# Sixteen column chunks instead of twelve in the opening of a decoder layer

## The chip, the cores and the metric

The kernel runs on one core of one Trainium2 chip. The metric is the time on the device of one launch, in microseconds (us). The figures used for comparison are medians over runs; the profile is of one further execution, and its own time stands beside its span below.

## What is computed

One layer with a batch of one, 256 positions, 2048 channels: a SwiGLU feed-forward block, a pair of token mixers (retention and windowed attention) and a second SwiGLU block, each behind an RMSNorm whose scale, shift and gate come from a conditioning vector `c`; then one last RMSNorm. The change touches the first block and the conditioning. Cut to that:

```python
mod = (silu(c) @ w_ada + b_ada).reshape(b, 9, 2048)          # w_ada: 2048 x 18432
h = rms_norm(x, norm_ffn1) * (1 + mod[:, 1]) + mod[:, 0]
gate, up = split(h @ w_ffn1_gu)                              # 2048 x 11264
x = x + 0.5 * mod[:, 2] * ((silu(gate) * up) @ w_ffn1_down)  # 5632 x 2048
h = rms_norm(x, norm_mix) * (1 + mod[:, 4]) + mod[:, 3]
# ... token mixing (mod 5), second feed-forward block (mod 6, 7, 8), last norm
```

Everything is float32. All weights are read from HBM once, about 595 MB.

## The kernel before

**Products.** A float32 product is made of three matmuls in a shorter format: each operand is split into a high and a low half, and high x high, low x high and high x low are summed in PSUM (`products`, lines 335 to 344; lines 342, 343 and 344 are the three). The 256 positions are two halves of 128, so one block of 128 weight rows times one chunk of 512 columns takes six matmuls. The weights are split as they come (`split`, lines 346 to 353): ScalarE casts two blocks at a time to the high half `wh` (line 350), VectorE subtracts to get the low half `wl` (line 352). The pool of these halves has three buffers for each. A raw load of weights lands in one of four buffers of four blocks, 1 MB each (`raws`, line 105).

**Conditioning.** For each of the nine vectors of `mod` and each of 16 blocks of 128 channels, a row of `w_ada` (1 MB, laid out with the channel on the partitions) is loaded (`ada_load`, line 197) and multiplied and summed on VectorE against `silu(c)` (`ada_pass`, line 203; its instruction is line 206, followed by a short read of the accumulator). In the opening a row takes two passes over 1024 columns; later it takes four over 512 (`AQ`).

**Opening (lines 867 to 993).** The normed input can only be used block by block, as the rows for `mod` 1 and 0 arrive. So the 16 blocks are put into groups, with `bounds` (line 931) of 2, 3, 3, 4 and 4 blocks. In each group twelve column chunks (`chunks`, gate and up chunks in turn, `2 * EARLY` of them) are visited once: `visit` (line 947) loads the group's blocks of that chunk and multiplies. There is PSUM for two chunks at a time (four accumulator banks). So between groups a chunk's sums go to SBUF (`to_parts`, line 965): the first time as a copy on ScalarE (line 970), later as an add on VectorE (line 968). `part_of` (line 873) says where: four chunks in each of three 16 KB slots. The order of chunks turns round with each group, and the last two chunks of a group stay in PSUM. In the last group `swiglu_up` (line 641) adds the partial sums (lines 651, 652), applies SiLU and multiplies (655), and transposes the result on TensorE (`transpose_to`, line 477, eight transposes for each pair of chunks).

While one group is visited, the rows of the next one are loaded and passed (`group`, line 900, a generator advanced after the visits, line 984). Its end transposes the normed input of the new blocks on TensorE (line 919), modulates on ScalarE (591, 596), and VectorE makes the low half of the activations (597). These rows use two half-slots in turn (`ring`).

**After the opening.** `ffn_up` (line 667) does the other chunk pairs over all 16 blocks at once, pairs 6 to 9 of eleven with the transposition done by DMA from SyncE (`turn_by_dma`, lines 484 to 510), over plane buffers (`flat`, `back`). Then comes the down product, whose activations are split into the pair buffers (`pair_tile`, line 357). After every two-block piece a `tick` (line 294) lets the generator `conditioning` (line 243) take some steps: it loads rows of `mod` 2, 4 and 3, up to `ahead` passes early, and passes them. `set_pace` (line 288) gives the steps per tick: 192 passes over 150 half-steps.

**Order.** SyncE issues the loads in program order, each when its buffer is free. The other engines' order is made by a scheduler at build time from the program order, except in parts written out by hand at the end of each down product.

Of the kernel before, what the change touches and what calls it, by code (L numbers as in the profile page):

```python
# [25 lines left out]
KB = 4  # L26
EPS = 1e-6
RAWS = 4
EARLY = 6

RH, RDK, RDV = 8, 128, 256
QH, KVH, HD = 32, 8, 64
# [45 lines left out]
def layer_kernel(  # L78
# [153 lines left out]
    def two_rows():  # L232

        both = slot()
        turn = [both[:, :D], both[:, D:]]

        def place():
            turn.append(turn.pop(0))
            return turn[-1]

        return place

    def conditioning(outputs, place, ahead, behind):


        tiles = [(m, k) for m, _, _ in outputs for k in range(KD)]
        held = {}
        step = 0
        for m, gain, row in outputs:
            sums = ada_sums()  # L250
            for k in range(KD):
                for q in range(AQ):
                    for i in range(step // AQ, min((step + ahead) // AQ + 1, len(tiles))):
                        if i not in held:
                            held[i] = place()
# [31 lines left out]

    def set_pace(outputs, halves, place, ahead):
        assert next(pace["steps"], None) is None
        pace["steps"] = conditioning(outputs, place, ahead, pace["behind"])  # L290
        pace["rate"] = len(outputs) * KD * AQ / halves
        pace["due"] = 0.0

    def tick():
        pace["due"] += pace["rate"]
# [50 lines left out]
    def split(pool, tag, src, n, hi_engine="act"):  # L346
        k = src.shape[1]
        hi = pool.tile([P, 2, n], F32R, tag=tag + "h", name=nm(tag + "h"))[:, :k, :]
        lo = pool.tile([P, 2, n], F32R, tag=tag + "l", name=nm(tag + "l"))[:, :k, :]
        cast.append(nc.scalar.copy(hi, src).ins)  # L350
        del cast[:-1]
        nc.vector.tensor_sub(lo, src, hi.bitcast(F32))  # L352
        return hi, lo
# [516 lines left out]
    tiles = [slot(), part[0]]  # L870
    ring = [tiles[0][:, :D], tiles[0][:, D:]]

    def part_of(n):
        at = (n % 4) * NT * CH
        return [part[n // 4][:, at + t * CH : at + (t + 1) * CH] for t in range(NT)]

# [51 lines left out]
    r = [Root(ssq, t).all() for t in range(NT)]  # L928
    for t in range(NT):
        nc.vector.tensor_scalar(out=r[t], in0=r[t], scalar1=HALF, scalar2=None, op0=ALU.mult)  # L930
    bounds = (0, 2, 5, 8, 12, 16)
    groups = [range(a, b) for a, b in zip(bounds, bounds[1:])]


# [9 lines left out]
        )  # L944
        return raw

    def visit(n, ks, raw, ends, step=2):
        starts = n not in banks
        if starts:
            banks[n] = [acc_bank() for _ in range(NT)]  # L950
        for a in range(0, len(ks), step):
            b = min(a + step, len(ks))
            hl = slice(ks[a], ks[a] + b - a)
            wh, wl = split(wsp, "w", raw[:, a:b, :], CH)
            products(
                banks[n],
                held.hi[:, hl, :],
                held.lo[:, hl, :],
                wh,
                wl,  # L960
                starts and a == 0,
                b == len(ks) and ends,
            )

    def to_parts(n):
        for p, b in zip(part_of(n), banks.pop(n)):
# [3 lines left out]
                nc.scalar.copy(p, b)  # L970
        moved.add(n)

    for _ in group(groups[0]):
        pass
    for g, ks in enumerate(groups):
        final = g == len(groups) - 1
        order = chunks if g % 2 == 0 else chunks[::-1]
        coming = iter(()) if final else group(groups[g + 1])
        due = 0 if final else 2 * len(groups[g + 1])
        stay = () if final else order[-2:]  # L980
        for i, n in enumerate(order):
            visit(n, ks, load_blocks(n, ks), n not in stay)
            last = len(order) - 2
            for _ in range((i + 1) * due // last - i * due // last if i < last else i == last):
                next(coming, None)
            if n in stay:
                continue
            if not final:
                to_parts(n)
            elif n % 2:  # L990
                swiglu_up(
                    banks.pop(n - 1), banks.pop(n), tiles, n // 2, (part_of(n - 1), part_of(n))
                )
    gate = gate_row()
    tiles.append(slot())
    place = two_rows()
    set_pace([(2, None, 0.5), (4, 1, None), (3, None, None)], 150, place, AQ)
    ffn_up(held, gu, tiles, EARLY, turned=range(EARLY, DFF // CH - 1))
    gate_load(gate, 2)
    wi = w_in[0]  # L1000
# [394 lines left out]
```

## Time and profile before

| | us |
|---|---|
| median of three runs | 2407.24 |
| lowest and highest | 2407.22, 2407.5 |
| profiled execution, its own time | 2406.89 |
| its span in the trace | 2404.9 |

| Engine | busy, us | share of the span |
|---|---|---|
| TensorE, matmul (PE) | 2369.5 | 99% |
| TensorE, weight load (PEld) | 1937.5 | 81% |
| VectorE (DVE) | 1694.8 | 70% |
| ScalarE (ACT) | 1293.9 | 54% |

In the profile's views a line names the engine, the source line (L352), the operation, the tiles written and read, their shapes and a count. A digit of the forty slices is the busy share in tenths of one fortieth of the span, about 60 us. "[1.66 <-PE pa L343]" behind an instruction says that its engine stood idle for 1.66 us before it, and that the wait ended when TensorE's line 343 had written the tile `pa`. A row of the view of waits has the waiting instruction, what ended the wait, and then total us, number of waits and the longest. Busy time is an average over stages: what a stage is worth is read from that stage.

### The profile page before, as it was taken

The page shows a single profiled execution, that of the slowest core. Times are in us where ns is not written, and L with a number is a line of the kernel's source. Part 1 is how long each engine was busy: PE and PEld are TensorE (multiplying, and loading weights), DVE is VectorE, ACT ScalarE, POOL GpSimd, SP SyncE. Part 2 cuts the span into 40 slices and gives each one's busy share as a digit, 9 for nine tenths or more (in the row PEclk, how much of TensorE's full clock was granted, in tenths as well). Part 3 has the DMA queues.
Part 4 walks back from the last instruction along what each step waited for, and adds up shares of the span by engine and source line. Part 5 has one row for each costly group of instructions (what it writes and reads, how often), then busy time and mean ns, then how long its engine had stood idle before and what let it go on. Part 6 is the DMA issues. An engine that isn't in the chain of part 4 may idle for free. (4 is left out here: it accounts for less than half of the span.)

```text
span 2404.9 us, 28941 instructions
## 1 busy us (share of the span) xinstructions
PE 2369.5 (99%) x10678; PEld 1937.5 (81%) x10678; DVE 1694.8 (70%) x2720; ACT 1293.9 (54%) x1799; POOL 5.7 (0%) x14
## 2 busy tenths in 40 slices
PE   6999999999999999999999999999999999999998
PEld 4778888888788887778888888887888888888886
DVE  7898787778877668886766766768655555545656
ACT  6544545454546456665555554456445445454544
POOL 0000000000000000000000000000000000000000
PEclk9999999999999999999999999999999999999999
DMA  9988688998876687775679787765677877875563
GB/s 354 341 327 286 230 309 301 374 321 310 299 263 227 228 283 226 223 230 210 218 252 290 264 282 265 278 197 203 221 239 238 247 255 241 260 221 188 184 205 126
DMA packets 307183, 614.28 MB, mean 255 GB/s; under 512 B 72737, under 2 KB 73121, under 8 KB 288225
## 3 DMA queue, kind: packets, MB, share of 16 engines
q1 hardware_dynamic: 305538, 605.78, 74.8%
q0 software_dynamic: 928, 5.61, 0.6%
q8 instruction: 84, 1.38, 0.2%
q10 hardware_dynamic: 576, 1.05, 0.1%
q14 instruction: 57, 0.47, 0.1%
HBM read 595.06 MB, written 2.12 MB: 248 GB/s over the span
## 5 line engine op out<-in xcount | busy, mean ns | idle before, releaser
L352 DVE TENSOR_TENSOR wl<-raw,wh 128x1024 fp32r<-128x1024 f32 (+1 forms) x806 | 968.2, 1207 | 560.4 <-ACT wh L350 555.6
L350 ACT CAST wh<-raw 128x1024 fp32r<-128x1024 f32 (+1 forms) x806 | 837.3, 1041 | 950.4 <-PE pa L343 932.7
L342 PE MATMUL pa<-wh,hh 128*128 128x512 f32 x2192 | 856.3, 392 | 2.3 <-ACT wh L350 1.8
L343 PE MATMUL pa<-wh,hl 128*128 128x512 f32 x2192 | 855.9, 391 | 2.1 <-DVE hl L597 2.1
L344 PE MATMUL pa<-wl,hh 128*128 128x512 f32 x2192 | 784.3, 392 | 2.5 <-DVE wl L352 2.4
L343 PEld LDWEIGHTS pa<-wh,hl 128*128 128x128 f32 x2192 | 411.9, 188 | 89.9 <-issue 3.0
L342 PEld LDWEIGHTS pa<-wh,hh 128*128 128x128 f32 x2192 | 411.6, 188 | 90.1 <-issue 2.8
L344 PEld LDWEIGHTS pa<-wl,hh 128*128 128x128 f32 x2192 | 409.1, 188 | 92.5 <-DVE wl L352 6.5
L343 PE MATMUL pa<-wh,a 128*128 128x512 f32 x944 | 365.1, 389 | 0.0
L342 PE MATMUL pa<-wh,a 128*128 128x512 f32 x944 | 350.0, 391 | 1.1 <-ACT wh L350 0.5
L344 PE MATMUL pa<-wl,a 128*128 128x512 f32 x944 | 349.0, 390 | 1.5 <-DVE wl L352 1.4
L344 PEld LDWEIGHTS pa<-wl,a 128*128 128x128 f32 x944 | 177.0, 188 | 40.2 <-DVE wl L352 3.5
L342 PEld LDWEIGHTS pa<-wh,a 128*128 128x128 f32 x944 | 177.1, 188 | 39.7 <-DVE slot L1277 1.0
L343 PEld LDWEIGHTS pa<-wh,a 128*128 128x128 f32 x944 | 177.1, 188 | 36.6 <-DVE a L385 0.2
L206 DVE CUSTOM_DVE_ANT_0 slot<-slot,cact 128x512 f32<-128x512 f32 (+1 forms) x252 | 192.8, 814 | 15.7 <-DMA slot<-in_w_ada_dram 15.6
L206 DVE CUSTOM_DVE_ANT_0 raw<-raw,cact 128x512 f32<-128x512 f32 (+1 forms) x260 | 167.1, 695 | 44.6 <-DMA raw<-in_w_ada_dram 33.9
L385 DVE TENSOR_TENSOR a<-slot,a 128x512 fp32r<-128x512 f32 x118 | 80.7, 685 | 1.7 <-ACT a L384 1.7
L508 ACT COPY slot<-back 128x512 uint16<-128x512 uint16 x116 | 77.1, 766 | 0.0
L384 ACT CAST a<-slot 128x512 fp32r<-128x512 f32 x118 | 72.7, 618 | 0.0
L494 ACT COPY flat<-t 128x512 uint16<-128x512 uint16 x104 | 58.9, 618 | 4.9 <-DVE t L1182 4.9
L206 DVE DVE_READ_ACCUMULATOR2_ANT sums<- 128x1 f32 x512 | 42.3, 83 | 0.0
L968 DVE TENSOR_TENSOR slot<-slot,pa 128x512 f32<-128x512 f32 x56 | 35.8, 681 | 0.0
(197 smaller groups left out, 1171.6 us busy)
## 6 DMA issues: line engine op xcount, KB each, us to landing
raw<-in_w_ffn_gu_dram SPq DMA_DIRECT2D x152, 1024.0 KB, 5.4
raw<-in_w_in_dram SPq DMA_DIRECT2D x104, 1024.0 KB, 5.3
raw<-in_w_ffn_down_dram SPq DMA_DIRECT2D x88, 1024.0 KB, 5.2
slot<-in_w_ada_dram SPq DMA_DIRECT2D x76, 1024.0 KB, 7.4
raw<-in_w_ada_dram SPq DMA_DIRECT2D x64, 1024.0 KB, 5.1
raw<-in_w_ffn_gu_dram SPq DMA_DIRECT2D x24, 768.0 KB, 7.2
raw<-in_w_swa_branch_dram SPq DMA_DIRECT2D x16, 1024.0 KB, 5.2
raw<-in_w_ret_branch_dram SPq DMA_DIRECT2D x16, 1024.0 KB, 5.2
```

The lines of the kernel that those rows point to most:

```text
L206: nc.vector.tensor_tensor_reduce(out=w[:, at], in0=w[:, at], in1=cact[:, at], scale=1.0, scalar=0.0, op0=ALU.mult, op1=ALU.add, accum_out= ...
L342: nc.tensor.matmul(ps, ah[:, j, ts], wh[:, j, :], start=first, stop=False)
L343: nc.tensor.matmul(ps, al[:, j, ts], wh[:, j, :], start=False, stop=False)
L344: nc.tensor.matmul(ps, ah[:, j, ts], wl[:, j, :], start=False, stop=last)
L350: cast.append(nc.scalar.copy(hi, src).ins)
L352: nc.vector.tensor_sub(lo, src, hi.bitcast(F32))
L384: nc.scalar.copy(hi, v)
L385: nc.vector.tensor_sub(lo, v, hi.bitcast(F32))
L494: nc.scalar.copy(planes[:, i, :], words(src)[:, :, i])
L508: nc.scalar.copy(into[:, :, :, i], held["turned"][:, i])
L968: nc.vector.tensor_add(p, p, b)
```

## The change

- `EARLY` becomes 8: sixteen chunks (eight pairs) in the opening, and `ffn_up` begins with pair 8. Pairs 6 and 7 are thus transposed on TensorE and no longer by DMA.
- The groups have 2, 4, 5 and 5 blocks. A visit with more than four blocks makes two loads, of three blocks and of the rest, and three pieces of 2, 1 and 2 blocks.
- The partial sums of chunks 12 and 13 are held in the two pair buffers, those of 14 and 15 in the four `back` plane buffers.
- In the last group each piece is followed by a `tick`, at a rate that takes 32 passes, which is eight of the later 48 rows. These rows (and the ninth) are placed in the raw load buffers, and are asked for one pass ahead. After the opening the rows go to two half-slots as before, and the other 160 passes are spread over 117 half-steps.
- The order of chunks begins reversed, so that the last group runs forward.

```diff
-EARLY = 6
+EARLY = 8
...
-                    for i in range(step // AQ, min((step + ahead) // AQ + 1, len(tiles))):
+                    for i in range(step // AQ, min((step + pace["ahead"]) // AQ + 1, len(tiles))):
...
+        pace["ahead"] = ahead
...
+    beside = [pair_tile() for _ in range(2)]
+    behind = [[back.tile([P, CH], F32, tag="back", name=nm("back")) for _ in range(NT)] for _ in range(2)]
+
     def part_of(n):
+        if n >= 14:
+            return behind[n - 14]
+        if n >= 12:
+            return [beside[n - 12][:, t, :] for t in range(NT)]
...
-    bounds = (0, 2, 5, 8, 12, 16)
+    bounds = (0, 2, 6, 11, 16)
...
-    def visit(n, ks, raw, ends, step=2):
+    def visit(n, ks, ends, ticks=False):
...
-        for a in range(0, len(ks), step):
-            b = min(a + step, len(ks))
-            hl = slice(ks[a], ks[a] + b - a)
-            wh, wl = split(wsp, "w", raw[:, a:b, :], CH)
+        cut = len(ks) if len(ks) <= KB else 3
+        raw_of = [(load_blocks(n, part), part) for part in (ks[:cut], ks[cut:]) if part]
+        pieces = [
+            (raw[:, a : a + 2, :], part[a : a + 2])
+            for raw, part in raw_of
+            for a in range(0, len(part), 2)
+        ]
+        for raw, part in pieces:
+            a, b = part[0] - ks[0], part[-1] + 1 - ks[0]
+            hl = slice(part[0], part[-1] + 1)
+            wh, wl = split(wsp, "w", raw[:, : len(part), :], CH)
...
+            if ticks:
+                tick()
...
+    ROWS_FFN1 = [(2, None, 0.5), (4, 1, None), (3, None, None)]
+    row_ring = []
+
+    def place_row():
+        return row_ring[0]() if row_ring else raw_row()
...
-        order = chunks if g % 2 == 0 else chunks[::-1]
+        if final:
+            set_pace(ROWS_FFN1, 48 * 192 // 32, place_row, 1)
+        order = chunks if (len(groups) - g) % 2 else chunks[::-1]
...
-            visit(n, ks, load_blocks(n, ks), n not in stay)
+            visit(n, ks, n not in stay, final)
...
-    place = two_rows()
-    set_pace([(2, None, 0.5), (4, 1, None), (3, None, None)], 150, place, AQ)
+    row_ring.append(two_rows())
+    pace["rate"] = (192 - 32) / 117
+    pace["ahead"] = AQ
     ffn_up(held, gu, tiles, EARLY, turned=range(EARLY, DFF // CH - 1))
```

More of the change, by code (lines that the diff above doesn't have):

```diff
@@ L241, in two_rows, with conditioning @@
         return place
-    def conditioning(outputs, place, ahead, behind):
+    def conditioning(outputs, place, behind):
         tiles = [(m, k) for m, _, _ in outputs for k in range(KD)]
@@ L289, in set_pace @@
         assert next(pace["steps"], None) is None
-        pace["steps"] = conditioning(outputs, place, ahead, pace["behind"])
+        pace["steps"] = conditioning(outputs, place, pace["behind"])
         pace["rate"] = len(outputs) * KD * AQ / halves
         pace["due"] = 0.0
+        pace["ahead"] = ahead
     def tick():
```

## The prediction

> **What bounds the kernel now.** I read the page first, for the engines' shares and the forty slices.
>
> ```profile
> span 2404.9 us, 28941 instructions
> PE 2369.5 (99%) x10678; PEld 1937.5 (81%) x10678; DVE 1694.8 (70%) x2720; ACT 1293.9 (54%) x1799; POOL 5.7 (0%) x14
> PE   6999999999999999999999999999999999999998
> PEld 4778888888788887778888888887888888888886
> DVE  7898787778877668886766766768655555545656
> ```
>
> TensorE (PE) sets the time nearly everywhere. Its row of nines hides small gaps, since the ends of matmuls are modelled; the weight-load row below it dips to 7 in slices 2 and 3 (60 to 180 us), just where VectorE (DVE) reads 8, 9 and 8. That is the opening, which the change rebuilds. So I next cut the opening into its five block groups.
>
> The cut comes from the timeline of ScalarE (ACT). The high-half buffers are three deep, so the cast of a piece waits for the last product of the piece three before it. Counting the casts (12 pieces in the first group, 24 in each later one), the cast three after a group's last piece marks that group's end on TensorE.
>
> ```profile
> 26.77 0.79 PE L342 MATMUL pa<-wh,hh 128*128 128x512 f32 x1 [0.81 <-ACT wh L350]
> ...
> 63.76 1.05 ACT L350 CAST wh<-raw 128x1024 fp32r<-128x1024 f32 x1 [0.18 <-PE pa L343]
> ...
> 113.51 1.05 ACT L350 CAST wh<-raw 128x1024 fp32r<-128x1024 f32 x1 [0.51 <-PE pa L343]
> ...
> 170.08 2.19 ACT L350 CAST wh<-raw 128x1024 fp32r<-128x1024 f32 x2 [0.62 <-PE pa L343]
> ...
> 238.24 1.05 ACT L350 CAST wh<-raw 128x1024 fp32r<-128x1024 f32 x1 [1.67 <-PE pa L343]
> ...
> 308.39 1.05 ACT L350 CAST wh<-raw 128x1024 fp32r<-128x1024 f32 x1
> ...
> 322.88 1.06 ACT L350 CAST wh<-raw 128x1024 fp32r<-128x1024 f32 x1 [1.68 <-PE pa L343]
> 325.60 1.06 ACT L350 CAST wh<-raw 128x1024 fp32r<-128x1024 f32 x1 [1.66 <-PE pa L343]
> 328.32 1.06 ACT L350 CAST wh<-raw 128x1024 fp32r<-128x1024 f32 x1 [1.66 <-PE pa L343]
> ```
>
> The third group's end is the second cast of the merged row, which ends at 172.27 after 1.06 us and so began at 171.21. The last three rows give the floor: 5.44 us for two pieces of two blocks each. One **unit** (one 128-row block of one column chunk, six products) costs 1.361 us of TensorE. The view of busy time by stretch, one row for each group and one for what follows (length, then busy time and count of PE, PEld, DVE, ACT, POOL, then clock, DMA share, GB/s):
>
> ```profile
> 26.77:63.75 36.98, 35.79 (x148) 28.19 (x149) 31.50 (x46) 27.43 (x45) 0.00 (x0) 1.00 1.01 386
> 63.75:113.51 49.76, 49.56 (x220) 40.62 (x219) 44.81 (x70) 24.69 (x37) 0.00 (x0) 1.00 0.90 330
> 113.51:171.21 57.70, 53.05 (x225) 40.16 (x224) 55.17 (x90) 26.02 (x41) 0.00 (x0) 1.00 0.88 323
> 171.21:238.24 67.03, 67.03 (x300) 55.01 (x299) 60.06 (x85) 32.35 (x44) 0.00 (x0) 1.00 0.84 306
> 238.24:308.38 70.14, 70.14 (x332) 58.28 (x331) 56.27 (x83) 39.87 (x51) 0.00 (x0) 1.00 0.67 227
> ```
>
> Floors are 24, 36, 36, 48 and 48 units: 32.7, 49.0, 49.0, 65.3 and 65.3 us. The excess is 4.3, 0.8, **8.7**, 1.7 and 4.8 us, 20.3 in all. The third group holds the loss worth having, and there VectorE is busy 55.17 of 57.70 us. One of its visits (a visit is one chunk times one group's blocks), on VectorE's timeline:
>
> ```profile
> 128.13 1.28 DVE L968 TENSOR_TENSOR slot<-slot,pa 128x512 f32<-128x512 f32 x2
> 129.32 1.22 DVE L352 TENSOR_TENSOR wl<-raw,wh 128x1024 fp32r<-128x1024 f32 x1
> 130.46 1.22 DVE L206 CUSTOM_DVE_ANT_0 slot<-slot,cact 128x1024 f32<-128x1024 f32 x1
> 131.60 0.08 DVE L206 DVE_READ_ACCUMULATOR2_ANT sums<- 128x1 f32 x1
> 131.60 1.22 DVE L206 CUSTOM_DVE_ANT_0 slot<-slot,cact 128x1024 f32<-128x1024 f32 x1
> 132.75 0.08 DVE L206 DVE_READ_ACCUMULATOR2_ANT sums<- 128x1 f32 x1
> 132.75 0.69 DVE L352 TENSOR_TENSOR wl<-raw,wh 128x512 fp32r<-128x512 f32 x1
> 133.35 1.28 DVE L968 TENSOR_TENSOR slot<-slot,pa 128x512 f32<-128x512 f32 x2
> ```
>
> From start to start: two adds into partial sums 1.19, a two-block split 1.14, a one-block split 0.60, one conditioning row (two passes) 2.29; the loop is 5.22 us against 4.08 (three units) on TensorE. Eight rows fall on the first ten visits, so the mean is 1.74 + 1.19 + 0.8 x 2.29 = 4.76 us, 0.68 over; ten visits lose 6.8 of the 8.7 us. The waits of that group show the rest:
>
> ```profile
> PE pa L343 <- DVE hl L597: 2.1, 2, 1.7
> PE pa L344 <- DVE wl L352: 2.0, 4, 0.8
> DVE slot L206 <- DMA slot<-in_w_ada_dram: 3.2, 2, 2.2
> ```
>
> VectorE stood 2.2 us at a row not yet landed at the boundary, and the low half of the activations (L597), queued behind it, was late. The fourth group has the same work at four blocks: 2.28 + 1.19 + 1.83 = 5.30 against 5.44, 97%, and loses only about 0.8 us beside its eight transposes. **So a group stalls when its visits are too narrow for the fixed work of rows and adds.**
>
> **The change, part by part.** *Wider groups and more chunks.* VectorE's need per visit, the same way (rows over the first 14 of 16 visits):
> - two blocks: 1.14 + 8/14 x 2.29 = 2.45 against 2.72 us (before 1.14 + 0.6 x 2.29 = 2.51);
> - four blocks: 2.28 + 1.19 + 10/14 x 2.29 = 5.11 against 5.44, 94%;
> - five blocks in pieces of 2, 1, 2: 2.88 + 1.19 + 1.64 = 5.71 against 6.80, 84%.
>
> The overload is gone from every group: of the 8.7 us, about 0.7 (six transposes) stays, 8.0 goes. The adds number 3 x 14 x 2 = 84 writes, 32 of them ScalarE copies, so 52 adds for 56 before: nothing. The pair and plane buffers are untouched until the first DMA turn and the down product, so holding partial sums there costs nothing; if a turn had to wait for one, TensorE would not, since its result is read by the down product. SyncE's issue of two loads per five-block visit is covered by 6.8 us of products.
>
> *First group.* It asks DMA for 0.524 + 0.571 x 1.049 = 1.12 MB per 2.72 us, 413 GB/s (before 0.524 + 0.6 x 1.049 = 1.15 MB, 424) where 386 were moved. The deficit lasts 14 visits instead of 10. Bounds: nothing (the old deficit is part of the 4.3), or 14 x (1.12/0.386 - 2.72) = 2.5 us. I take **0.5 us** more than the 4.3 of now, as the missing 27 GB/s make 1.0 MB over 38 us, as the 38 GB/s of now do over 27 us.
>
> *The last group.* Eight pairs of chunks turn on TensorE instead of six, two fewer by DMA.
>
> ```profile
> 257.10 0.40 PE L343 MATMUL pa<-wh,hl 128*128 128x512 f32 x1
> 257.34 1.04 PE L477 MATMUL ps<-small_c,t 128*128 128x128 f32 x8
> 258.13 0.47 PE L344 MATMUL pa<-wl,hh 128*128 128x512 f32 x1
> ```
>
> Eight transposes push the next product from 257.33 to 258.13: 0.80 us. Two more pairs cost **1.6 us**, surely on the path. VectorE there also gets eight rows, at two short passes a visit:
>
> ```profile
> L651 DVE TENSOR_TENSOR t<-pa,slot 128x512 f32<-128x512 f32 x12 | 7.9, 687 | 2.7 <-PE pa L344 2.7
> L206 DVE CUSTOM_DVE_ANT_0 slot<-slot,cact 128x512 f32<-128x512 f32 x12 | 7.6, 685 | 0.0
> ```
>
> Three such operations (0.66) and two passes (0.63 + 0.08): 2.88 + 1.98 + 1.42 = 6.3 against 6.8 + 0.4, 87%. It fits, but is no longer slack: a split waits behind a pass, and a pass behind its row. The rows now take one of the four load buffers, in SyncE's order between the weights. The trace has such rows only later in the kernel:
>
> ```profile
> DVE raw L206 <- DMA raw<-in_w_ada_dram: 33.9, 27, 3.1
> raw<-in_w_ada_dram SPq DMA_DIRECT2D x64, 1024.0 KB, 5.1
> raw<-in_w_ffn_gu_dram SPq DMA_DIRECT2D x10, 1024.0 KB, 5.0
> raw<-in_w_ffn_gu_dram SPq DMA_DIRECT2D x24, 768.0 KB, 7.2
> ```
>
> VectorE waits for 64 such rows 33.9 us in 27 waits, 0.5 a row, at most 3.1. (The last two rows are weights: 225 to 280 us and 25 to 302 us, with the median time to landing at the end.) Bounds for eight rows: nothing, or 8 x 3.1 = 25 us, of which 16 x 0.9 = 14 is cover, so 11. I take **1.2 us**, the kinder end, because SyncE reaches a row's load about a visit ahead of its first pass, longer than the 5.0 us that a load takes from 225 us on, where the group moved 227 GB/s (the changed stage asks for 1.84 MB per 7.2 us, 255 GB/s).
>
> *Boundaries.* Three instead of four, but up to five blocks are modulated at each. Bounds: nothing (the last boundary of now), or the 2.1 us of the third group's, each. I take 0.8 for the four-block group and 0.4 for the next, as the fourth group's 0.8 at 97%.
>
> *Later.* Forty rows over 117 half-steps instead of 48 over 150: 1.37 passes per step against 1.28. That is 0.09 x 0.7 us more per 2.72 us, covered where VectorE has most to do:
>
> ```profile
> 650.00:700.00 50.00, 49.31 (x214) 39.98 (x215) 43.73 (x77) 25.05 (x35) 0.00 (x0) 1.00 0.81 295
> ```
>
> VectorE is still idle for an eighth of that stretch; nothing to 1 us, I take nothing. The 64 units moved into the opening cost 1.361 each on either side.
>
> **Sum.** Against 20.3: 8.0 and about 0.8 (the fourth group's stall) go; 0.5, 1.6, 1.2, 0.8 and 0.4 come, 4.5 in all: a gain of **4.3 us**. The span becomes 2400.6. The profiled execution took 2406.89 with its span of 2404.9, and the median is 2407.24, 2.3 over the span: **2402.9 us**.
>
> **A rule against it.** In the first group, whose weight loads are of 512 KB, the engines moved 386 GB/s; in the second, of 768 KB, 330. The Trainium skill ("DMA: Bandwidth & Descriptors", "Rules for kernel authors") asks for at least 1 MiB in one DMA for full bandwidth, and a five-block visit here is cut into 0.75 and 0.5 MiB. By the rows the smallest loads stood beside the highest rate, so the sum takes nothing for it; by the rule these loads land late, which is the slower rival below.
>
> **Rivals.**
> *The load buffers run short (slower).* With a row in one of four, a visit's first load waits for the buffer of the visit before, which is free once that visit's second piece is split. Its cast goes when the second piece of the visit before that ends, 4.08 us into 7.2; with the cast (0.6), the split (0.6) and one other vector operation ahead (1.2) the buffer is free at 6.5, 7.9 us before the load's own visit. Less a cast of 1.06 and a split of 1.14, 5.7 us remain for landing. At 5.0 all is well; at 7.2, as the 768 KB loads took where groups moved 323 to 386 GB/s, each of eight row periods loses 1.5: 12.0 us, less the 1.2 counted, so 10.8 lost against 4.3 won: **2414 us**. For it: the two landing times lie on both sides. Against: the stage asks for 255 GB/s only.
>
> *The stall moves to the boundaries (no change).* If late rows and late halves, not visit width, made the third group's loss, each of three boundaries costs about 2.7 us (8.0 over the third group's one is the extreme); 8 - 1.2 = 6.8 more than counted would leave 2410, half of it **2406**. For it: the 2.1 and 2.2 us rows. Against: 5.22 against 4.08 within the group.
>
> *Nothing new stalls (better).* The first group costs no more, last group and boundaries lose nothing, and the 0.7 us idle at 650 to 700 goes too: 4.3 + 2.9 + 0.7 = 7.9: **2399 us**.
>
> **How the numbers follow.** Forecast 0.52 (its own range 2400 to 2405), boundaries 0.20, better 0.13, buffers short 0.15. The range that leaves out about 2 in 10 is 2397 to 2411. I call 0.2%, 4.8 us, what a measurement can tell from none. Faster by that needs under 2402.4: the better case (0.13), nearly half of the forecast (0.25) and 0.02 of the boundary case, 0.40; slower, over 2412, most of the buffer case with a little beyond the boundary one, 0.14; the rest, 0.46.
>
> **What would show it.** In the changed trace: four groups near 48, 89, 110 and 116 us; in the four- and five-block groups casts that wait for TensorE every piece; VectorE under 95% in each; row waits of some tenths in the last group. Wrong, if a group's excess over its units is above 4 us past the first, if weights' casts wait for DMA in the last group (buffers short), or if L597 holds TensorE at boundaries.

## The result, and the profile after

The change makes the kernel slower, where a gain of 4.3 us was forecast.

| | before | after |
|---|---|---|
| median, us | 2407.37 (8 runs) | 2413.61 (8 runs) |
| lowest and highest, us | 2406.85, 2408.61 | 2409.72, 2417.31 |
| profiled execution, its own time, us | 2406.89 | 2413.91 |
| its span in the trace, us | 2404.9 | 2412.1 |

The ratio is 1.0027, with a 95% interval from 1.0018 to 1.0036. The runs also scatter more: 7.6 us between the extremes against 1.8.

Line numbers move by one behind line 29 and by more later: the three products are lines 343 to 345 here, the cast is 351, the low half 353. Two of the costliest groups on the page of the changed kernel (line, engine, operation, tiles, count, then busy us, mean ns, and idle time before them with what ended it):

```profile
L345 PE MATMUL pa<-wl,hh 128*128 128x512 f32 x2192 | 784.3, 392 | 8.1 <-DVE wl L353 7.9
...
L206 DVE CUSTOM_DVE_ANT_0 raw<-raw,cact 128x512 f32<-128x512 f32 (+1 forms) x292 | 187.4, 695 | 74.1 <-DMA raw<-in_w_ada_dram 63.4
```

TensorE's idle time before the third product rose from 2.5 to 8.1 us, nearly all of it for low halves, and VectorE's wait for rows in load buffers from 33.9 to 63.4. Where that is, the same cut by groups shows. The ends of the four groups, read from ScalarE's casts as in the prediction:

```profile
75.74 1.05 ACT L351 CAST wh<-raw 128x1024 fp32r<-128x1024 f32 x1 [0.18 <-PE pa L344]
...
163.88 1.05 ACT L351 CAST wh<-raw 128x1024 fp32r<-128x1024 f32 x1 [2.10 <-PE pa L344]
...
276.95 1.06 ACT L351 CAST wh<-raw 128x1024 fp32r<-128x1024 f32 x1 [1.45 <-PE pa L344]
...
401.32 1.04 ACT L351 CAST wh<-raw 128x1024 fp32r<-128x1024 f32 x1 [2.46 <-DMA raw<-in_w_ffn_gu_dram]
```

The last of them was released by a load and not by TensorE, so that end is an upper bound. By TensorE's own records the next piece's first product starts at 400.50; where a cast is released by TensorE the two lie 0.03 us apart, so the last group ends at 400.47. The view by stretch (columns as in the prediction):

```profile
26.57:75.74 49.17, 47.18 (x196) 37.04 (x197) 41.50 (x58) 35.91 (x57) 0.00 (x0) 1.00 1.00 382
75.74:163.88 88.14, 88.14 (x393) 72.72 (x392) 76.60 (x106) 40.65 (x52) 0.00 (x0) 1.00 0.84 309
163.88:276.94 113.06, 110.94 (x495) 91.21 (x494) 93.14 (x134) 53.32 (x76) 0.00 (x0) 1.00 0.78 277
276.94:401.32 124.38, 118.18 (x543) 95.93 (x542) 97.69 (x169) 62.84 (x83) 0.00 (x0) 1.00 0.73 251
```

The floors are 32, 64, 80 and 80 units of 1.3605 us (the prediction's 1.361): 43.5, 87.1, 108.8 and 108.8. The excess is 5.6, 1.1, 4.2 and **14.7 us** (15.5 up to the cast), 25.6 in all against 20.3 before. The overload of VectorE is gone as computed (it is busy 87% and 82% of the second and third group), but the last group has taken the loss. Its waits:

```profile
DVE raw L206 <- DMA raw<-in_w_ada_dram: 22.3, 7, 5.3
PEld pa L345 <- DVE wl L353: 8.6, 6, 3.0
PE pa L345 <- DVE wl L353: 6.2, 4, 2.6
```

VectorE waits seven times, 3.2 us each, for a row that has not landed, and TensorE then waits for the low half that is queued on VectorE behind the row's passes. One such place on VectorE, the wait of TensorE that follows, and the same time on SyncE:

```profile
297.28 1.82 DVE L353 TENSOR_TENSOR wl<-raw,wh 128x1024 fp32r<-128x1024 f32 x2
299.02 1.28 DVE L652 TENSOR_TENSOR t<-pa,slot 128x512 f32<-128x512 f32 x2
300.38 1.23 DVE L353 TENSOR_TENSOR wl<-raw,wh 128x1024 fp32r<-128x1024 f32 x1
306.23 0.69 DVE L206 CUSTOM_DVE_ANT_0 raw<-raw,cact 128x512 f32<-128x512 f32 x1 [4.62 <-DMA raw<-in_w_ada_dram]
...
308.07 0.69 DVE L206 CUSTOM_DVE_ANT_0 raw<-raw,cact 128x512 f32<-128x512 f32 x1
...
308.69 1.82 DVE L353 TENSOR_TENSOR wl<-raw,wh 128x1024 fp32r<-128x1024 f32 x2
...
309.96 0.73 PE L345 MATMUL pa<-wl,hh 128*128 128x512 f32 x2 [1.88 <-DVE wl L353]
```

```profile
299.13 0.34 SPq L201 DMA_DIRECT2D raw<-in_w_ada_dram  x1
301.63 11.60 SPq L949 DMA_DIRECT2D raw<-in_w_ffn_gu_dram  x4
315.81 0.34 SPq L201 DMA_DIRECT2D raw<-in_w_ada_dram  x1
```

The row's load is issued at 299.13, just when VectorE's split at 297.28 to 299.10 has freed a load buffer. VectorE has 2.5 us of other work left, then reaches the row's first pass at 301.61, and stands until 306.23: the row took 7.1 us from issue to its first pass. All four passes stand together, so a late row holds up all that follows: the next split starts at 308.69, and TensorE stands 1.88 us for it.

### The profile page after: what moved, and what is told of

The parts are those of the page before. It is cut to its first block, busy times and chain, and to the rows that moved or that the text cites. A ratio compares the mean times of both kernels' runs of the same rounds, so it can differ in the third digit from the quotient of the medians.

```text
span 2412.1 us, 29026 instructions
## 1 busy us (share of the span) xinstructions
PE 2370.4 (98%) x10694; PEld 1939.2 (80%) x10694; DVE 1698.2 (70%) x2723; ACT 1291.1 (54%) x1799; POOL 5.7 (0%) x14
## 5 line engine op out<-in xcount | busy, mean ns | idle before, releaser
L206 DVE CUSTOM_DVE_ANT_0 raw<-raw,cact 128x512 f32<-128x512 f32 (+1 forms) x292 | 187.4, 695 | 74.1 <-DMA raw<-in_w_ada_dram 63.4
L206 DVE CUSTOM_DVE_ANT_0 slot<-slot,cact 128x512 f32<-128x512 f32 (+1 forms) x220 | 172.3, 830 | 6.6 <-DMA slot<-in_w_ada_dram 6.4
L509 ACT COPY slot<-back 128x512 uint16<-128x512 uint16 x108 | 71.8, 766 | 0.0
L1115 ACT ACTIVATE a<-a,ng 128x128 f32<-128x128 f32 (+1 forms) x64 | 28.4, 446 | 9.1 <-DVE ng L1101 9.1
```

Source lines behind the costliest of these rows:

```text
L206: nc.vector.tensor_tensor_reduce(out=w[:, at], in0=w[:, at], in1=cact[:, at], scale=1.0, scalar=0.0, op0=ALU.mult, op1=ALU.add, accum_out= ...
L509: nc.scalar.copy(into[:, :, :, i], held["turned"][:, i])
L1115: nc.scalar.activation(seg, seg, AF.Exp, bias=ng[:, z : z + 1], accum_out=sm[:, z : z + 1])
```

## The experiments

All runs build on the changed kernel except where stated. For each, the table has the median, its ratio to the kernel before, run beside it, with the 95% interval, and the excess of each group over its units in its profile, read as above. A star marks a last group whose cast was released by a load and whose end is therefore read from TensorE's records. "Later" is the excess of the 96 pieces (192 units, 261.2 us) after the opening, read at the cast; with twelve chunks these pieces are other work, so that column compares the versions with sixteen.

| run | median | ratio | groups | later |
|---|---|---|---|---|
| before | 2407.4 | | 4.3, 0.8, 8.7, 1.7, 4.8 | |
| the change | 2413.6 | 1.0027 (1.0018 to 1.0036) | 5.6, 1.1, 4.2, 14.7* | 5.3 |
| no rows | 2407.4 | 1.0000 (0.9991 to 1.0010) | 6.7, 1.1, 3.4, 6.6 | 6.9 |
| passes tied to pieces | 2412.2 | 1.0018 (1.0009 to 1.0028) | 7.1, 1.1, 6.1, 7.7* | 9.3 |
| resident row | 2418.5 | 1.0045 (1.0030 to 1.0060) | 8.4, 1.1, 10.7, 6.9 | 4.6 |
| low halves first | 2420.9 | 1.0052 (1.0037 to 1.0067) | 6.7, 1.1, 4.8, 19.5* | 7.2 |
| old groups | 2408.9 | 1.0004 (0.9995 to 1.0014) | 2.6, 2.8, 3.6, 1.6, 5.7 | 17.2 |
| groups alone | 2412.7 | 1.0021 (1.0011 to 1.0030) | 14.6, 2.5, 3.0, 5.1 | |
| half-slots | 2404.8 | 0.9989 (0.9980 to 0.9999) | 7.1, 1.1, 6.1, 10.2 | 1.8 |
| half-slots and held passes | 2403.7 | 0.9981 (0.9971 to 0.9990) | 6.1, 1.0, 1.7, 10.1 | 1.8 |
| slower rows, tied | 2414.0 | 1.0030 (1.0018 to 1.0041) | 5.6, 1.0, 1.7, 16.7* | 5.4 |
| old groups, tied | 2414.5 | 1.0030 (1.0018 to 1.0041) | 3.2, 0.6, 5.0, 2.7, 7.0* | 12.1 |
| fewer rows, not tied | 2404.1 | 0.9986 (0.9977 to 0.9995) | 5.7, 1.0, 1.7, 7.2 | 4.2 |
| old groups, not tied | 2410.3 | 1.0011 (1.0002 to 1.0019) | 1.8, 0.6, 5.1, 2.7, 6.1 | 10.0 |

The columns of groups and "later" are of one execution each. That of "old groups" took 2416.0 us, the longest of its ten, so its "later" is above the usual; that of "half-slots" took 2408.2 us, 3.4 above its median, and that of "fewer rows, not tied" 2402.0, the shortest of its eleven and 2.1 below.

### No rows in the last group

```diff
-        if final:
-            set_pace(ROWS_FFN1, 48 * 192 // 32, place_row, 1)
...
-            visit(n, ks, n not in stay, final)
+            visit(n, ks, n not in stay)
...
+    set_pace(ROWS_FFN1, 117, two_rows(), AQ)
```

> Sixteen chunks and groups 2, 4, 5, 5 as in the change, but no later row in the last group: all 192 passes of the 48 later rows are spread over the 117 half-steps after the opening (1.64 a step instead of 1.37). Theory (VectorE waits in the last group for rows whose load was issued only some 3 us before): the last group falls from 124.4 to about 116 us (108.8 for its units, 6.7 for transposes), VectorE waits for no row there, and the runs scatter less than the 8 us of the changed kernel; the later stage, at 1.14 + 0.34 + 1.64 x 0.71 = 2.64 of 2.72 us a step on VectorE, may lose 1 to 4 us, so 2404 to 2409 us. If the last group were bound by its two weight loads a visit or by adds and splits alone, it stays above 120 us.

The view by stretch, last group:

```profile
277.90:393.31 115.41, 115.41 (x539) 96.10 (x538) 82.60 (x110) 63.41 (x83) 0.00 (x0) 1.00 0.65 209
```

It takes 115.4 us, 6.6 over its units, most of it the transposes (the trace lists 58 there, 0.10 us each). The rows in the last group thus cost 8 us there (14.7 less 6.6). The time is still that of the kernel before, as the later stage, with 1.64 passes a step, gives the gain back: at the same piece of work, counted in ScalarE's casts from the end of the trace, this version is 2.2 us ahead of the kernel before with 650 casts to go (some 40 us behind the opening) and 0.9 us behind with 500 to go, as it is at the end. Denser rows cost about 3 us there.

### Passes tied to their pieces

```diff
+                    if pace["hold"]:
+                        with tc.issue_after(lows[-1]):
+                            ada_pass(k, held[step // AQ], sums, q)
```

`lows[-1]` is the last low half of a weight piece; `hold` is set in the last group.

> The change with one edit: in the last group each pass is tied behind the low half of the piece before its tick on VectorE, so the four passes of a row keep the order of the program instead of standing in one burst. Theory (late row, because the burst stands right behind the landing that the build's scheduler assumed): the row has one to two pieces more to land, its wait falls from 22.3 to under 8 us, and the last group from 124.4 to 118 to 120 us; 2408 to 2411 us. Rival (the four load buffers are short): a row now holds its buffer for two visits, weights come later, the casts wait for their loads and the last group stays at 124 us or over.

The waits of its last group (casts are line 354 here):

```profile
DVE raw L206 <- DMA raw<-in_w_ada_dram: 10.8, 6, 2.3
...
ACT wh L354 <- DMA raw<-in_w_ffn_gu_dram: 8.9, 3, 3.0
```

VectorE's wait for rows halved, from 22.3 to 10.8 us, and casts waited 8.9 us for weights, as the rival expected. But TensorE hardly felt it. The cast behind this group waited for a load until 402.16, while TensorE began the next piece at 396.67; up to there the view by stretch shows it busy throughout, and behind it stand a wait of VectorE and one of TensorE:

```profile
280.08:396.64 116.56, 116.56 (x539) 95.83 (x538) 92.76 (x155) 61.90 (x83) 0.00 (x0) 1.00 0.75 250
```

```profile
396.98 0.69 DVE L206 CUSTOM_DVE_ANT_0 slot<-slot,cact 128x512 f32<-128x512 f32 x1 [2.50 <-DMA slot<-in_w_ada_dram]
...
400.71 0.73 PE L348 MATMUL pa<-wl,hh 128*128 128x512 f32 x2 [2.98 <-DVE wl L356]
```

So the group takes 116.6 us, 7.7 over its units against 14.7 in the change and 6.6 without rows, below the expected 118 to 120. The rows and their load buffers are the change's own; the edit moves only the passes on VectorE (31 stand in this group, 36 in the change's). That shows the cause of the last group's loss: the place of the passes, ahead of low halves that TensorE needs next. The whole gains only 1.4 us by the medians. In the profile the first and third group lost 3.4 us more than the change's, for which no cause was sought, and the later stage 4.0 more: it begins with a row in a half-slot, no longer tied, whose four passes stand ahead of a low half (the last two rows).

### A resident row

```diff
-                            held[i] = place()
-                            ada_load(*tiles[i], held[i])
+                            held[i] = pace["resident"] or place()
+                            if not pace["resident"]:
+                                ada_load(*tiles[i], held[i])
```

> The change with the eight row loads of the last group left out: its 32 passes are all made, but on one row that was loaded into an idle buffer during the first group (so conditioning vector 2 is not the reference's for eight blocks). VectorE's work stays, load and buffer use go. Theory (waiting for late rows): last group 116 to 118 us, about 2405 us. Rival (VectorE's work of passes, adds and splits overfills the group): it stays above 121 us, 2411 us or more.

The view by stretch, third and last group, and the passes on the resident row in each:

```profile
168.58:288.15 119.57, 113.26 (x497) 91.25 (x496) 106.51 (x184) 54.25 (x79) 0.00 (x0) 1.00 0.74 254
288.15:403.88 115.73, 115.44 (x537) 95.85 (x536) 85.48 (x119) 62.45 (x81) 0.00 (x0) 1.00 0.66 211
```

```profile
L206 DVE CUSTOM_DVE_ANT_0 row<-row,cact 128x512 f32<-128x512 f32 x29 | 19.4, 708 | 0.0
...
L206 DVE CUSTOM_DVE_ANT_0 row<-row,cact 128x512 f32<-128x512 f32 x4 | 2.7, 715 | 0.0
```

The last group has the expected 115.7 us, but not for the expected reason: with the data at hand, the scheduler put nearly all the passes into the third group, where they keep VectorE busy for 19.4 us and the excess is 6.5 us above the changed kernel's. VectorE's waits for rows there are 6.2 us against 4.9, so most of the 6.5 is work. The run doesn't tell waiting from work in the last group. It shows another thing: passes cost TensorE time even when their own row is not waited for.

### Low halves of the activations first

```diff
+                    if made and k == ks[0]:
+                        with tc.issue_after(made[0]):
+                            ada_pass(k, rows_of[m, k], early[m], q, passes)
+                        continue
```

`made[0]` is the last low half of the activations that was made before.

> The change with one edit at the group boundaries: the first block's passes of the next group are tied behind the last low half of the activations (VectorE's line 598) instead of standing ahead of it. Theory: VectorE's wait of 3.4 us for a row at the boundary of the second and third group no longer delays the low halves, and the third group falls from 113.1 to about 111 us; the last group stays near 124; about 2 us off the whole. Rival (the low halves are late because ScalarE makes the high ones late): the third group stays at 113.

The low halves are no longer waited for, but the third group stays (113.6 us), since VectorE waits for later rows instead. In the last group rows were waited for as before, a little longer:

```profile
DVE slot L206 <- DMA slot<-in_w_ada_dram: 8.6, 7, 2.1
...
DVE raw L206 <- DMA raw<-in_w_ada_dram: 25.5, 7, 5.1
```

The first row is of the third group, the other of the last. The expectation failed in both groups. The last one lost 4.8 us more than in the changed kernel; 1.7 of this is a stretch of 3.4 us from 311.8 us in which the granted clock was 0.50, and the rest was not followed further.

### Sixteen chunks, old groups

```diff
-    bounds = (0, 2, 6, 11, 16)
+    bounds = (0, 2, 5, 8, 12, 16)
```

on the run without rows.

> Sixteen chunks with the old five groups of 2, 3, 3, 4 and 4 blocks, no later row in the opening (192 passes over 117 half-steps, as in the run without rows). By VectorE's count a three-block visit needs 1.74 + 1.19 + 8/14 x 2.29 = 4.24 us against 4.08, where twelve chunks needed 4.76. Theory (the third group's loss was visits too narrow for the fixed work): it loses 14 x 0.16 = 2.2 us plus 0.7 for transposes, about 3 us instead of 8.7, and the opening's excess is 15 to 17 us. Rival (that loss came from late rows at boundaries): the third group still loses 7 us or more. The whole 2405 to 2409 us, since the later stage is as dense as in the run without rows.

The third group's excess is 3.6 us where twelve chunks had 8.7, close to the 2.9 of the count, and the opening's excess is 16.3. The visits are as wide as before and the boundary is the same; only the rows are spread over fourteen visits instead of ten. So VectorE's load in each visit, not the boundary, made most of the old loss.

### The groups alone, twelve chunks

```diff
-EARLY = 8
+EARLY = 6
...
-    set_pace(ROWS_FFN1, 117, two_rows(), AQ)
+    set_pace(ROWS_FFN1, 150, two_rows(), AQ)
```

on the run without rows.

> Twelve chunks as before, with the groups of 2, 4, 5 and 5 alone, no later row in the opening (192 passes over 150 half-steps, as before the change). By count the first group asks DMA for 0.524 + 0.8 x 1.049 = 1.36 MB per 2.72 us where 386 GB/s were moved, so it loses 10 x 0.8 = 8 us more than the 4.3 of before; the four-block group needs 2.28 + 1.19 + 2.29 = 5.76 against 5.44 on VectorE, 3 us; the five-block group 6.36 against 6.80, so only late rows cost it. Theory: excess about 12, 4, 2 to 4 and 6 us, 24 to 26 in all against 20.3; 2410 to 2413 us. If the first group loses no more than 6 us, DMA does not set its pace.

The first groups of this run and of the one with old groups:

```profile
26.18:73.47 47.29, 41.82 (x161) 30.57 (x161) 39.28 (x58) 28.69 (x49) 0.00 (x0) 1.00 0.99 381
...
26.41:72.55 46.14, 46.14 (x194) 37.93 (x195) 36.21 (x49) 33.12 (x54) 0.00 (x0) 1.00 0.95 354
```

With 501 GB/s asked for, the engines move 381 and the group loses 14.6 us; with 358 asked for, they move 354 and it loses 2.6. In these runs DMA sets the first group's pace when about 380 GB/s or more are asked for. The four-block group lost 2.5 us (expected 3 and transposes).

### Half-slots, then held passes

```diff
-        if final:
-            set_pace(ROWS_FFN1, 48 * 192 // 32, place_row, 1)
...
-            visit(n, ks, n not in stay, final)
+            if final and i == 10:
+                row_ring.append(two_rows())
+                set_pace(ROWS_FFN1, 117 + 18, place_row, AQ)
+            visit(n, ks, n not in stay, final and i >= 10)
```

and for the second of the two, in the opening's own rows:

```diff
+                    if lows:
+                        with tc.issue_after(lows[-1]):
+                            ada_pass(k, rows_of[m, k], early[m], q, passes)
+                        continue
```

> The change with its later rows begun only with the eleventh of sixteen visits of the last group, in two half-slots (those of the partial sums of chunks 4 to 11, which are free by then) and a whole row ahead, as after the opening; 192 passes over 18 + 117 half-steps, 1.42 a step. No row takes a load buffer. Theory (rows were late because each waited for one of four load buffers): no row wait over 1 us in the last group, which takes 116 to 118 us, and the later stage loses 1 to 2 us instead of the 3.8 more of the run without rows: 2403 to 2406 us. Rival (a row's own landing time is the trouble wherever it is put): waits of 2 to 5 us a row again, and 119 us or more.

> The run before this one in the list, and the opening's own passes tied behind the low half of the last piece before them, so that none stands earlier on VectorE than in the program's order. Theory (the scheduler at build time puts a pass where it supposes the row landed, which is too early on the chip): VectorE's waits for slot rows in the third group, 4.9 us in the changed kernel, fall under 1.5 us and the group's excess from 4.2 to about 2 us; first and second group as they are; 2401 to 2404 us. Rival (rows are late in the program's order too, as SyncE issues them late): the waits stay, or the splits behind them are later, and the third group keeps 3 us or more.

Third and last group of the second one, and the passes of its last group:

```profile
164.61:275.18 110.57, 110.57 (x493) 91.09 (x492) 91.97 (x128) 51.83 (x72) 0.00 (x0) 1.00 0.81 276
275.18:394.12 118.94, 117.86 (x545) 96.59 (x544) 96.16 (x160) 63.86 (x87) 0.00 (x0) 1.00 0.77 261
```

```profile
L206 DVE CUSTOM_DVE_ANT_0 slot<-slot,cact 128x512 f32<-128x512 f32 x32 | 20.4, 683 | 0.6 <-DMA slot<-in_w_ada_dram 0.6
```

The last group makes 32 passes of later rows, the changed kernel 36, with 0.6 us of waiting instead of 23.0, and takes 118.9 instead of 123.5 us. With the waiting, 4.6 of the 8 us are gone. The other 3.5 stay: the expected 116 to 118 was missed. Holding the opening's passes to the program's order took the third group's excess from 6.1 to 1.7, as expected; its waits for rows, 9.3 us in the run without the tie, are gone. Of the 6.1, some 1.7 us are a stretch at half the clock (last section); in four profiles with the same groups and no such tie the third group lost 3.4 to 6.1 us, with the tie 1.7 in all three. By the medians the tie brought 1.1 us, and the two intervals overlap.

### Slower rows, and the old groups again

The first ties the last group's passes to their pieces too, and slows them; the second does so with the old groups; the last two do without that tie.

```diff
-                set_pace(ROWS_FFN1, 117 + 18, place_row, AQ)
+                set_pace(ROWS_FFN1, 117, place_row, AQ)
+                pace["rate"], pace["hold"] = 16 / 18, True
...
+    pace["rate"], pace["hold"] = (192 - 16) / 117, False
```

> The version with half-slots and held passes (2403.7 us), with fewer and slower rows in the last group: 16 passes over its last 18 ticks instead of 25, each tied behind the low half of its piece, and 1.50 instead of 1.42 passes a half-step afterwards. There VectorE's rows stood in bursts of up to eight passes and the group took 118.95 us, 10.1 over its units of which 6.7 are transposes. Theory (those 3.4 us are VectorE's: 2.88 + 1.98 + 3 x 1.42 x 0.71 = 7.9 us a visit against 7.2): at 2.88 + 1.98 + 3 x 0.89 x 0.71 = 6.8 the group falls to 116 us, and the later stage loses 0 to 2 us more; 2401 to 2403 us. Rival (the loss is the row loads in SyncE's order, ahead of weights): it stays at 118 us or more and the whole at 2403 to 2405.

> The same with the old five groups of 2, 3, 3, 4 and 4 blocks (12 passes in the last 12 ticks of the last group, 1.54 a half-step afterwards). From the run with old groups: first group 2.6 us over its units instead of 6.1, as it asks DMA for 358 GB/s instead of 413; the three-block groups about 2.8 and 3.6; with held passes the second of these may fall to 3. Theory (DMA sets the first group, VectorE's count the others): excess about 2.6, 2.8, 3, 1.5 and 6.5, 16 to 17 in all against 19 with wide groups, so 2400 to 2403 us. Rival (the held passes undo the three-block groups, whose visits have no slack on VectorE, 4.24 against 4.08): 8 us and more in the second and third group, 2405 us or more.

Both failed. SyncE's waits in the last group of the first (L957 is a weight load, L201 a row), ScalarE's wait for weights there, and TensorE's longest:

```profile
SPq L957 <- DVE wl L356: 55.4, 19, 4.0
SPq L201 <- DVE sums L206: 46.6, 5, 12.0
```

```profile
ACT wh L354 <- DMA raw<-in_w_ffn_gu_dram: 9.1, 3, 4.1
```

```profile
391.24 0.80 PE L346 MATMUL pa<-wh,hh 128*128 128x512 f32 x1 [5.37 <-ACT wh L354]
```

SyncE issues in order. A row's load that waits up to 12 us for its half-slot, because the passes that free it were slowed, holds back the weight loads behind it. The group took 125.5 us by TensorE's records, with VectorE less busy than before (91.5 us against 96.2). So the tie that helped the third group, and the last one while its rows were in load buffers, hurts here, and the version is no better than the change. In the second, with the old groups, the last group was near what was expected (7.0 us), but the later stage lost 12.1.

> The version with half-slots and the opening's passes held (2403.7 us), with 16 passes instead of 25 in the last group's 18 ticks and 1.50 a half-step afterwards, and without the tie of the last group's passes that the run with slower rows had (there four row loads waited 44.1 us on SyncE for their half-slots, with the weights' loads behind them). Theory (rows that stand early in bursts free their half-slot before SyncE comes to the next row's load, and fewer of them leave VectorE room): no cast waits over 2 us for a weight load, last group 116 to 118 us instead of 118.95, later stage at most 1.5 us worse, 2402 to 2404 us. Rival (the half-slots hold up SyncE at any lower pace, tied or not): weight casts wait for DMA 5 us or more, group over 120.

> The same with the old five groups, 16 passes in the last 12 ticks of the last group. The first group as in the other runs with these groups, 2.6 to 3.2 us over its units instead of 6.1; second and third about 0.6 and 5; fourth 1.5 to 2.7. Theory: without the tie the last group, 12.3 with it, comes to 7 to 9 us, 18 to 20 in all, level with the wide groups: 2403 to 2406 us. Rival (the later stage at 1.50 a half-step is what costs, as the two runs with 1.54 and 1.64 lost 10.8 and 15.7 us there by their profiles): 2408 us or more.

Third and last group of the version with fewer rows, and the passes of its last group:

```profile
163.97:274.52 110.55, 110.55 (x493) 91.09 (x492) 92.01 (x128) 51.78 (x72) 0.00 (x0) 1.00 0.82 276
274.52:390.58 116.06, 115.95 (x541) 96.22 (x540) 92.22 (x144) 63.85 (x87) 0.00 (x0) 1.00 0.72 244
```

```profile
L206 DVE CUSTOM_DVE_ANT_0 slot<-slot,cact 128x512 f32<-128x512 f32 x24 | 15.4, 688 | 0.3 <-DMA slot<-in_w_ada_dram 0.3
```

With 24 passes and hardly any waiting the last group is at 116.06 us, 0.6 over the run without rows: the rest of the loss was VectorE's passes. That it was their standing in bursts and not their number is argued only from the tied run above, which had 31 of them, spread over the group, at 116.6. What this version wins there the later stage gives back (4.2 against 1.8 us), and 2404.1 us is level with the 2403.7 of the version with more rows. Both are faster than the kernel before by 0.1 to 0.2%, with intervals clear of 1. No run tied the passes of both places with the rows in load buffers.

With the old groups the row loads also wait for the half-slots themselves. SyncE's waits in the not tied one of these, from 298 to 400 us:

```profile
SPq L201 <- DVE sums L206: 27.9, 7, 7.9
SPq L201 <- DVE t L657: 13.9, 1, 13.9
```

A visit there needs one load, so four buffers take SyncE four visits ahead, to the rows of visit 11 while the partial sums in their slot are still read (L657). The opening's excess is only 16.2 us, but the later stage loses 10.0, and the run is slower, as its rival said. (Counted as in the table, the two runs that it cites lost 12.1 and 17.2 us there; it says 10.8 and 15.7.)

## Why the prediction was wrong

**The overload of VectorE, 8.0 us gone: right.** The run with old groups shows the count at work (3.6 us at 4.24 against 4.08, where 4.76 gave 8.7), and the four-block group of the change is 1.1 us over its units, transposes included.

**The last group, 1.2 us: the step that failed.** The prediction argued that SyncE reaches a row's load about a visit (7.2 us) ahead of its first pass, and took the kind end of 0 to 11 us. The trace shows 2.5 us between issue and the moment when VectorE comes to the pass, for two reasons that were not looked for: the row takes the buffer that the visit just before it frees, and the scheduler puts the four passes in one burst early on VectorE instead of spreading them over two visits by ticks. The cost was 14.7 less 6.6, some 8 us. The second reason made most of it: with the passes tied to their pieces, and the buffers as they were, the group fell to 7.7. The first alone made rows wait there too (10.8 us in six waits on VectorE), but TensorE hardly felt them. The version with half-slots, which changes the storage and the pace of the rows and leaves the bursts, won 4.6 of the 8.

**First group, 0.5 us: too small.** It was 1.3 in the changed kernel, and 1.3 to 2.8 in the others with the same rows and weights ahead of it. The mechanism was right: DMA sets it.

**Boundaries, 0.4 for the five-block group: too small.** The third group lost 4.2, of which 1.4 are its fourteen transposes, so 2.8 us. It was again rows not yet landed (4.9 us of VectorE's waits); TensorE stood 2.1 us for the low half of the activations (line 598 here), one of the prediction's signs of being wrong. The tie to the program's order took the group to 1.7 us.

**The four-block group, 0.8: slightly too much**; it was 0.3 beside its eight transposes.

**Later, nothing: right for the stage that it was said of.** The two kernels at the same piece of work, ScalarE's cast number 400 and number 300 from the end (of line 350, 351 after the change), before and after:

```profile
1231.88 1.04 ACT L350 CAST wh<-raw 128x1024 fp32r<-128x1024 f32 x1
...
1505.21 1.05 ACT L350 CAST wh<-raw 128x1024 fp32r<-128x1024 f32 x1 [1.15 <-PE pa L343]
```

```profile
1237.71 1.04 ACT L351 CAST wh<-raw 128x1024 fp32r<-128x1024 f32 x1
...
1512.35 1.05 ACT L351 CAST wh<-raw 128x1024 fp32r<-128x1024 f32 x1 [1.15 <-PE pa L344]
```

The change is behind by about 6 us once the opening is over (25.6 of excess against 20.3, and 0.8 us of waiting for a low half in the first piece behind it) and by 5.8 at the first of these, so nothing more was lost in the first feed-forward block. It is behind by 7.1 at the second and by 7.2 at the end: 1.3 us come between 1232 and 1512 us, in the token mixing, which the change doesn't touch. VectorE's passes on rows in load buffers, 1300 to 1520 us of the kernel before and of the change (columns of the groups):

```profile
L206 DVE CUSTOM_DVE_ANT_0 raw<-raw,cact 128x512 f32<-128x512 f32 x60 | 37.9, 687 | 6.6 <-DMA raw<-in_w_ada_dram 6.6
```

```profile
L206 DVE CUSTOM_DVE_ANT_0 raw<-raw,cact 128x512 f32<-128x512 f32 x56 | 35.4, 687 | 10.4 <-DMA raw<-in_w_ada_dram 10.3
```

Rows were waited for longer there, 10.3 against 6.6 us. Which of them TensorE felt, and why, no run took apart.

**The corrected sum.** By spans, as the groups were read: 2400.6 forecast + 7.1 (last group, 14.7 where 4.8 + 1.6 + 1.2 were forecast) + 0.8 (the piece behind it) + 0.8 (first group) + 1.7 (the two groups between, 5.3 where 3.6 were forecast) + 1.3 (token mixing) - 0.2 (the opening starts at 26.57 instead of 26.77) = 2412.1, the span of the profile. As these figures are read from that profile, the agreement shows that no large term is missing, and no more.

**Transposes, 1.6 us: right.** Without rows the last group is 6.6 us over its units, 1.8 more than the 4.8 of before.

**The rivals.** The slower rival gave 2414 us, near the result, but by luck and not by its mechanism: it expected weight loads to be late for want of buffers. In the changed kernel the row was late for that want. The loads that it blamed are cleared by their times to landing in the last group, against the 5.7 us that it left them (count, size, median us). The Trainium skill ("DMA: Bandwidth & Descriptors", "Rules for kernel authors") asks for at least 1 MiB in one DMA for full bandwidth; no median of the smaller loads was late here:

```profile
raw<-in_w_ffn_gu_dram SPq DMA_DIRECT2D x14, 768.0 KB, 5.4
raw<-in_w_ffn_gu_dram SPq DMA_DIRECT2D x14, 512.0 KB, 3.6
raw<-in_w_ada_dram SPq DMA_DIRECT2D x7, 1024.0 KB, 5.9
```

The 386 GB/s of the first group say less about small loads than the prediction took from them: of the loads issued there before the change, six were rows of 1 MB, five weights of 768 KB and eight of 512 KB. The boundary rival named the right kind of stall for the third group, at a smaller price. The better case, 2399 us, was reached by no version.

## What to carry to other kernels

When work that waits for a load moves to a new place, don't ask how far ahead its load stands in the program, but which event frees the buffer that the load needs, and how much of the waiting engine's own work lies between that event and the wait; here it was 2.5 us against a landing of about 6. A share of spare time on an engine (13% on VectorE in the last group by the prediction's count) doesn't cover work that stands in bursts ahead of what the bound engine needs next: the same passes in the program's order cost that group about 1 us instead of 8. And with all loads in one in-order queue, any slowing of the work that frees a buffer holds up every load behind the one that waits for it.

## What was not expected of the hardware

The changed kernel scattered over 7.6 us in eight runs, the kernel before over 1.8 in the same comparison (over 5.1 in another, of 31 runs). VectorE's waits for rows do not explain it: "half-slots" scattered over 8.1 us with hardly a wait for rows in its last group (9.3 us of them in its third), and "low halves first", with the longest such waits (25.5 us), over 2.6 in four runs. One part of it shows in the traces. Seven times between 20 and 2390 us, in five of the profiles, the granted clock was 0.50 for 3.4 us, and each time within 1.6 us of the end of a wait of TensorE of 1.7 to 5.4 us. In "half-slots" it came behind the wait of 2.2 us at 171.28:

```profile
172.10:175.50 3.40, 3.40 (x11) 2.63 (x10) 1.29 (x3) 1.23 (x3) 0.00 (x0) 0.50 0.94 345
```

Half the clock for 3.4 us costs 1.7 us of products. Not every such wait brings it: 2.56 us in the change and 3.04 in "passes tied to pieces" had none behind them. In "half-slots" the three executions with a mean clock under 0.999 are the three longest. What decides, and what else scatters, is open.

One edit had opposite signs. Tying VectorE's passes to the program's order took the third group's excess from 6.1 to 1.7 us ("half-slots" against "half-slots and held passes"); in the last group the same tie, at the same rate of rows, took it from 7.2 to 16.7 ("fewer rows, not tied" against "slower rows, tied"; 1.7 of this is the half clock). It is not the group that decides: with rows in load buffers the tie took the last group from 14.7 to 7.7. In the bad case SyncE, which issues in order, waited up to 12 us for the half-slot that the tied passes free.
